# Seventeen of twenty-two gate and up pairs of a SwiGLU block as seven half-size products, with two weight sums made by accumulating transfers

## The chip, the cores and the metric

The kernel runs on one core of one Trainium2 chip. The metric is the device time of one execution in microseconds (us); the kernel before was run three times, and its median is the figure to compare with. A separate, profiled execution left the trace from which every row below is read. TensorE is called PE, VectorE DVE, ScalarE ACT, GpSimd POOL and SyncE SP, as in the profile.

## The reference, cut to what matters

Two transformer blocks run one after the other on 512 tokens of width 1024, all in fp32. Block 1 mixes with a multi-scale pool and a dilated attention and then has a SwiGLU layer of width 2816; block 2 mixes with three attentions and ends with other gated layers. The change is in block 1's SwiGLU, the first half of it:

```python
h = rms_norm(x, ln_pre_ffn[l])
f = (jax.nn.silu(h @ w_gate[l]) * (h @ w_up[l])) @ w_down[l]
x = x + rms_norm(f, ln_post_ffn[l])
```

`h` is 512 x 1024, `w_gate` and `w_up` are 1024 x 2816. The result must hold fp32 accuracy.

## The kernel before

Activations lie transposed: features on the 128 partitions, the 512 tokens along the free axis. The 2816 columns of gate and of up are cut into 22 blocks of 128; block i of gate and block i of up are a pair, and each of the two is a slab: eight chunks of 128 input features, and for each chunk three matmuls, since fp32 accuracy is had from a reduced format (fp32r) by splitting every operand into a high and a low part: high x high, high x low, low x high (`mm3`, L186 to L188). A slab is thus 24 matmuls of 128x128 weights with 128x512 tokens, a pair 48.

Weights come in units of 512 KB (one slab of 128 columns). SP starts the load into one of two buffers of the pool `raw` (L158); ACT makes the high part by a rounding copy (L164), DVE the low part by a subtraction (L167), in two halves of 128x512, into rings of ten buffers each (`NW`). An SP queue runs in order, and a load into a `raw` buffer waits until the parts of the unit before in that buffer are made.

`ffn1` makes the pairs in a loop. The first two pairs (four slabs) are interleaved chunk by chunk and by token halves (`beside`); after that each slab stands by itself. When the slabs of a pair are done, DVE multiplies gate by the row of inverse norms R (L647), ACT applies silu (L112), DVE multiplies up by R (L650) and both together (L651), and the product is split for the down projection (ACT L176, DVE L177) and kept in the slots `p`, `t`, `o`, `k`. R is applied after the matmuls, so that `h` there is not yet normed. The down projection (`post`) follows.

A list scheduler orders the instructions of each engine when the kernel is built; at run time each engine and each queue goes strictly in that order. Slots are named buffer classes with a count (`SLOTS`); PSUM has eight banks of 128x512.

Of the kernel before, what the change touches and what calls it, by code (L numbers as in the profile page):

```python
# [21 lines left out]
EPS = 1e-6  # L22
BIG = 1e30
WH = 524
# [5 lines left out]
NW = 10  # L30
# [12 lines left out]
DONE2 = [0, 1, 2, 3, 4, 5, 6, 7]  # L43
KA2 = 6
BESIDE = 4
NA2 = 4
SLOTS = dict(h=16, o=14, k=16, z=6, v=8, p=8, t=6, m=8)

# [13 lines left out]
class Builder:  # L62
# [118 lines left out]
                lo[:, cols], src[:, cols], scale, hi[:, cols].bitcast(F32), ALU.mult, ALU.subtract)  # L181
        return hi, lo

    def mm3(self, out, ahi, alo, bhi, blo, start, stop):
        mm = self.nc.tensor.matmul
        mm(out, lhsT=ahi, rhs=bhi, start=start, stop=False)  # L186
        mm(out, lhsT=ahi, rhs=blo, start=False, stop=False)  # L187
        mm(out, lhsT=alo, rhs=bhi, start=False, stop=stop)  # L188

    def slab(self, out, name, s, h, order=None, halves=((0, S),), units=None, gate=None, free=0):  # L190
        order = list(range(len(h))) if order is None else order
# [228 lines left out]
    def setup(self):  # L420
        nc = self.nc
        self.res = None
        self.special = []
        self.mark = None
        self.tables("natural_log_exp_and_others")
        io = self.io
        self.cols = self.const("cols", [P, NCOL])
        self.ident = self.const("ident", [P, P])
        self.ones = self.const("ones", [P, P])
        self.eps = self.const("eps", [P, 1])  # L430
        self.one = self.const("one", [P, 1])
        nc.sync.dma_start(self.cols[:, :KD], io["cols"][:, :KD])
        self.rest = lambda: nc.sync.dma_start(self.cols[:, KD:], io["cols"][:, KD:])
        nc.gpsimd.memset(self.ones, 1.0)
        warm = self.psT()
        for _ in range(WARM):
            nc.tensor.matmul(warm[:, 0:P], lhsT=self.ones, rhs=self.ones, start=True, stop=True)
        nc.gpsimd.memset(self.eps, EPS)
        nc.gpsimd.memset(self.one, 1.0)

    def load_x(self, ks=range(KD)):
        x = []
        for k in ks:
            t = self.slot("v")
            self.load_late(t, self.io["x"][k])
            x.append(t)
        return x

# [88 lines left out]
    def pool_branch(self, us, oT):  # L537
        nc = self.nc
        io = self.io
        add = ALU.add  # L540
        hi, lo = self.wunit("w_pool", 0, 1)[0]

        def shift_add(src, k, rows=slice(0, P)):
            t = self.slot("h")
            nc.vector.tensor_tensor(t[rows, k:], src[rows, k:], src[rows, :S - k], add)
            nc.vector.tensor_copy(t[rows, :k], src[rows, :k])
            return t
        for i in range(2):
# [12 lines left out]
            ps = self.psum()  # L561
            c = slice(i * P, i * P + P)
            self.mm3(ps, hi[:, c], lo[:, c], dh, dl, True, True)
            oT[i] = self.split(ps, self.col("pool_scale", i), tag="k")

    def post(self, a, order, wname, gname, nname, rows):
        nc = self.nc
        get = self.units(wname)
        acc = self.slot("z")
        mg = []  # L570
        x = self.res
        H = (slice(0, 256), slice(256, S))
        R = self.slot("z")
        nk = len(a)

        def part(m, cols, gate=None):
            d = self.psum(True)
            if m == len(mg):
                mg.append(self.slot("m"))
            self.slab(d, wname, m, a, order, ((cols.start, cols.stop),), get,  # L580
                      gate, (GATE if nk == KD else GATE2) if m == cut else 0)
            nc.scalar.activation(mg[m][:, cols], d[:, cols], AF.Copy, scale=self.col(gname, m))
            self.square_acc(acc, d, m == 0, cols)
        cut = KD - (NHALF if nk == KD else NHALF2)
        for m in range(cut):
            part(m, slice(0, S))
        if x is None:
            x = self.load_x()
        self.res = x
        h = self.h_tiles()  # L590
# [24 lines left out]

    def h_tiles(self):
        return [(self.slot("h", F32R), self.slot("h", F32R)) for _ in range(KD)]

    def stats(self, rows, tag="z"):
        acc = self.slot(tag)  # L620
# [8 lines left out]
    def ffn1(self, h, R):  # L629
        nc = self.nc  # L630
        self.tables("silu_and_others")
        get = self.units("w_gu1")
        act = []
        for i in range(KF):
            if i == 0:
                early = [self.psum(True) for _ in range(BESIDE)]
                self.beside(early, range(BESIDE), h, ((0, 256), (256, S)), get)
            gu = []
            for s in (2 * i, 2 * i + 1):
                if s < BESIDE:  # L640
# [11 lines left out]
            act.append(self.split(t, **self.act_tiles(i)))  # L652
        self.tables("natural_log_exp_and_others")
        return self.post(act, None, "w_down", "ln_post_ffn", "ln_mix_2", False)

    def mix2(self, h, rc):
        nc = self.nc
# [222 lines left out]
    def ffn2(self, h, R):  # L880
# [113 lines left out]
def _layout(i):  # L994
# [80 lines left out]
```

## Time and profile before

| what | value |
|---|---|
| three runs | 1343.4, 1339.58, 1339.52 us, median 1339.58 us |
| the profiled execution | 1343.58 us, its span 1341.5 us |
| PE busy | 1311.8 us of the span (98%) |
| DVE busy | 851.3 us (63%) |
| ACT busy | 672.6 us (50%) |
| POOL busy | 153.8 us (11%) |
| mean granted TensorE clock | 0.994 of full |
| seventeen pairs that the change touches | 292.4 to 481.6 us after the span's start |

The times are on one axis from the span's start. The span is 2.1 us shorter than its own execution; those 2.1 us lie before the first and after the last instruction. Instructions of one engine overlap a little: the time from one start to the next is what an instruction takes away from its engine, and the duration is longer, as it runs to the last result.

### The profile page before, as it was taken

The page shows a single profiled execution, that of the slowest core. Times are in us where ns is not written, and L with a number is a line of the kernel's source. Part 1 is how long each engine was busy: PE and PEld are TensorE (multiplying, and loading weights), DVE is VectorE, ACT ScalarE, POOL GpSimd, SP SyncE. Part 2 cuts the span into 40 slices and gives each one's busy share as a digit, 9 for nine tenths or more (in the row PEclk, how much of TensorE's full clock was granted, in tenths as well). Part 3 has the DMA queues.
Part 4 walks back from the last instruction along what each step waited for, and adds up shares of the span by engine and source line. Part 5 has one row for each costly group of instructions (what it writes and reads, how often), then busy time and mean ns, then how long its engine had stood idle before and what let it go on. Part 6 is the DMA issues. An engine that isn't in the chain of part 4 may idle for free.

```text
span 1341.5 us, 20064 instructions
## 1 busy us (share of the span) xinstructions
PE 1311.8 (98%) x7450; PEld 1138.0 (85%) x7450; DVE 851.3 (63%) x1771; ACT 672.6 (50%) x1327; POOL 153.8 (11%) x190
## 2 busy tenths in 40 slices
PE   9799999999999999999999999899999999999998
PEld 9799988988888888888988999779888888888887
DVE  7777885864444432229588878766877777733354
ACT  6466755543333332237576777755554444522241
POOL 1232220000000000001222334430000000000000
PEclk9999999999999999999999999999999999999999
DMA  6322334233333333228244445333332332332221
GB/s 228 109 67 68 95 111 126 70 117 96 96 95 95 94 95 94 95 70 262 88 112 117 123 117 138 93 106 124 126 95 95 94 95 94 102 95 94 94 79 63
DMA packets 48801, 141.69 MB, mean 106 GB/s; under 512 B 6240, under 2 KB 7136, under 8 KB 48704
## 3 DMA queue, kind: packets, MB, share of 16 engines
q1 hardware_dynamic: 48704, 140.42, 34.0%
q8 instruction: 58, 0.95, 0.3%
q14 instruction: 39, 0.32, 0.1%
HBM read 122.38 MB, written 6.29 MB: 96 GB/s over the span
## 4 chain that ended last, share of the span: by engine, by line
PE 84%; DVE 8%; DMA 3%; ACT 2%; issue 2%; SPq 1%; POOL 0%; DVEq 0%; ACTq 0%; POOLq 0%
PE p L186 21%; PE p L187 21%; PE p L188 21%; PE p L372 4%; PE p L373 4%; PE p L374 4%; DVE wl L167 2%; PE p L283 2%; PE p L292 1%; PE p L291 1%; PE p L261 1%; DVE sp L265 1%; PE p L262 1%; DMA wr<-in_w_qk 1%; ACT sp L112 1%
## 5 line engine op out<-in xcount | busy, mean ns | idle before, releaser
L164 ACT ACTIVATE wh<-wr 128x512 fp32r<-128x512 f32 x417 | 259.2, 630 | 405.4 <-PE p L187 351.9
L167 DVE TENSOR_TENSOR wl<-wr,wh 128x512 fp32r<-128x512 f32 (+1 forms) x400 | 286.2, 723 | 238.5 <-ACT wh L164 227.1
L188 PE MATMUL p<-sh,wl 128*128 128x512 f32 (+1 forms) x858 | 320.4, 377 | 0.0
L187 PE MATMUL p<-sh,wh 128*128 128x512 f32 (+1 forms) x858 | 319.5, 376 | 0.1
L186 PE MATMUL p<-sh,wh 128*128 128x512 f32 (+1 forms) x858 | 311.0, 375 | 1.0 <-ACT sh L179 0.7
L372 PE MATMUL p<-wh,sh 128*128 128x256 f32 (+1 forms) x672 | 193.3, 289 | 5.8 <-ACT sz L485 3.3
L373 PE MATMUL p<-wl,sh 128*128 128x256 f32 (+1 forms) x672 | 192.1, 287 | 0.3 <-DVE wl L167 0.2
L374 PE MATMUL p<-wh,sh 128*128 128x256 f32 (+1 forms) x672 | 191.2, 286 | 0.0
L187 PEld LDWEIGHTS p<-sh,wh 128*128 128x128 f32 x858 | 161.2, 188 | 32.6 <-issue 0.5
L188 PEld LDWEIGHTS p<-sh,wl 128*128 128x128 f32 x858 | 161.2, 188 | 31.8 <-issue 0.7
L186 PEld LDWEIGHTS p<-sh,wh 128*128 128x128 f32 x858 | 157.2, 188 | 33.4 <-ACT sh L179 1.1
L372 PEld LDWEIGHTS p<-wh,sh 128*128 128x128 f32 x672 | 128.7, 192 | 9.1 <-ACT sz L485 3.6
L373 PEld LDWEIGHTS p<-wl,sh 128*128 128x128 f32 x672 | 128.9, 192 | 1.1 <-DVE wl L167 0.8
L374 PEld LDWEIGHTS p<-wh,sh 128*128 128x128 f32 x672 | 128.6, 192 | 1.1 <-issue 0.5
L273 POOL TENSOR_SCALAR sp<-sp,m 128x128 f32<-128x128 f32 (+1 forms) x112 | 72.0, 647 | 186.3 <-DVE m L269 145.5
L112 ACT ACTIVATE sp<-sp,m 128x128 f32<-128x128 f32 (+3 forms) x128 | 71.5, 560 | 36.4 <-DVE m L265 33.8
L188 PE MATMUL p<-so,wl 128*128 128x512 f32 (+1 forms) x246 | 88.5, 360 | 0.0
L187 PE MATMUL p<-so,wh 128*128 128x512 f32 (+1 forms) x246 | 88.5, 360 | 0.0
L186 PE MATMUL p<-so,wh 128*128 128x512 f32 (+1 forms) x246 | 87.6, 361 | 0.6 <-DVE m L265 0.5
L167 POOL TENSOR_TENSOR wl<-wr,wh 128x512 fp32r<-128x512 f32 (+1 forms) x17 | 23.8, 1402 | 455.3 <-ACT wh L164 443.7
L265 DVE CUSTOM_DVE_ANT_0 sp<-p,sm 128x128 f32<-128x128 f32 (+3 forms) x128 | 60.4, 483 | 17.3 <-PE p L262 13.5
L187 PE MATMUL p<-sk,wh 128*128 128x512 f32 (+1 forms) x184 | 67.1, 365 | 0.0
(205 smaller groups left out, 2138.8 us busy)
## 6 DMA issues: line engine op xcount, KB each, us to landing
wr<-in_w_gu SPq DMA_DIRECT2D x88, 512.0 KB
wr<-in_w_down SPq DMA_DIRECT2D x44, 512.0 KB
wr<-in_w_qk SPq DMA_DIRECT2D x31, 512.0 KB
sk<-sk SPq DMA_DIRECT2D x88, 128.0 KB
wr<-in_w_out SPq DMA_DIRECT2D x12, 512.0 KB
sv<-in_x SPq DMA_DIRECT2D x16, 256.0 KB
wr<-in_w_ple_gate SPq DMA_DIRECT2D x8, 512.0 KB
wr<-in_w_v SPq DMA_DIRECT2D x6, 512.0 KB
```

The costliest lines, as they stand in the source:

```text
L112: i = self.nc.scalar.activation(out, in_, func, **k)
L164: nc.scalar.activation(hi[:, :w], c, AF.Copy)
L167: eng.tensor_tensor(lo[:, :w], c, hi[:, :w].bitcast(F32), ALU.subtract)
L186: mm(out, lhsT=ahi, rhs=bhi, start=start, stop=False)
L187: mm(out, lhsT=ahi, rhs=blo, start=False, stop=False)
L188: mm(out, lhsT=alo, rhs=bhi, start=False, stop=stop)
L265: nc.vector.tensor_tensor_reduce(p[:, :n], ps[:, :n], tab[:, (3 - qb) * P:S], 1.0, 3e38, ALU.add, ALU.min, accum_out=m[:, 0:1])
L273: self.nc.gpsimd.tensor_scalar(p[:, :n], p[:, :n], m[:, 2:3], 1.0, ALU.mult, ALU.mult)
L283: ins = nc.tensor.transpose(pt[:, w:w + P], ps_list[qb][:, kb * P:kb * P + P], self.ident)
L372: mm(d, lhsT=h[k][0][:, a], rhs=hi[:, c], start=k == 0 and (o == 0 or not first), stop=False)
L373: mm(d, lhsT=h[k][0][:, a], rhs=lo[:, c], start=False, stop=False)
L374: mm(d, lhsT=h[k][1][:, a], rhs=hi[:, c], start=False, stop=k == 7 and (o > 0 or not first))
```

## The change

Pairs 0 to 4 (`PLAIN = 5`) stay as they were. Pairs 5 to 21, seventeen of them, are computed by Strassen's scheme in its form with seven products. The two-by-two blocks are: first and second half of the input features (four chunks each), first and second half of the tokens (256 each), and gate against up. Of the weights g1, g2 (halves of gate) and u1, u2 (halves of up) seven left operands are made: g1, s1 = u1 + u2, s2 = s1 + g1, g2, s3 = g1 + u1, u2, s4 = s2 + g2. Of the four quarters of the normed `h` seven right operands are made once for all pairs (`h_forms`). Each product has four chunks of three matmuls of 128x128 weights with 128x256 tokens: 84 matmuls of half width for a pair, in place of 48 of full width. The products are summed partly in PSUM (products 0, 2, 4 and 5 in one bank, 1 and 6 in another, 3 in a third) and partly by DVE on 128x256 blocks.

For every such pair DVE now has seven low parts of 128x512 (`L788`), two sums s2 and s4 (`L779`), five additions or multiplications of 128x256 (L693, L697, L701, L705, L707) and one split; ACT has seven high parts (`L787`), three copies out of PSUM of 128x256, two silus of 128x256 and one split. The sums s1 and s3 are made by transfers: SP loads one addend of 256 KB into a buffer (`L768`), and POOL then starts a transfer of the other addend, 256 KB, that adds into that buffer (`L769`). Gate is loaded whole (512 KB, `L771`) and u2 as 256 KB (`L775`), both into the two `raw` buffers, so that gate always takes the same one. The four buffers s1 to s4 are single and are used by all seventeen pairs. A pair moves 1.79 MB in place of 1.0 MB. `h` is normed ahead of the products in place of R behind them.

Once, during pairs 1 to 3, DVE and ACT make the right operands: 16 products of 128x256 (L738), 8 sums or differences of 128x512 (L747) and 14 splits. To have room, the residual x is written to DRAM (`parked`, eight transfers of 256 KB, L638) and loaded again in `post`; the unnormed `h` of the plain pairs moves to slots `k`, and one result of the pool branch to slots `h`. The scheduler also orders some pieces of block 1's mixing tail and of block 2's attention a little differently.

```diff
-        for i in range(KF):
+        self.parked = self.dp.tile([KD, P, S], F32, tag="parked", name="parked")
+        for m in range(KD):
+            nc.sync.dma_start(self.parked[m], self.res[m])
...
+        for i in range(PLAIN):
...
+            if i == 0:
+                forms, todo = self.h_forms(R)
+                each = -(-len(todo) // (PLAIN - 2))
+            else:
+                for step in todo[(i - 1) * each:i * each]:
+                    step()
+        self.res = None
+        sums = [self.slot("m") for _ in range(4)]
+        late = []
+        for i in range(PLAIN, KF):
+            wf = self.w_forms(2 * i, sums)
+            A, B, C = (self.psum(True) for _ in range(3))
+            half = slice(0, 256)
+            e, f, t = self.slot("z"), self.slot("z"), self.slot("z")
...
+                    self.mm3(out[:, half], hi[:, c], lo[:, c], bh[:, a], bl[:, a], first and k == 0, k == 3, True)
+
+            times(A, 0, True)
+            nc.scalar.activation(e[:, half], A[:, half], AF.Copy)
+            times(C, 1, True)
+            for step in late[:1]:
+                step()
+            times(A, 2)
+            nc.scalar.activation(e[:, 256:], A[:, half], AF.Copy)
+            for step in late[1:]:
+                step()
+            times(B, 3, True)
+            nc.vector.tensor_tensor(t[:, half], B[:, half], e[:, half], ALU.add)
+            self.act(t[:, half], t[:, half], AF.Silu)
+            times(A, 4)
+            nc.scalar.activation(f[:, half], A[:, half], AF.Copy)
+            nc.vector.tensor_tensor(f[:, 256:], C[:, half], f[:, half], ALU.add)
+
+            def left(A=A, t=t, times=times):
+                times(A, 5)
+                nc.vector.tensor_tensor(t[:, half], t[:, half], A[:, half], ALU.mult)
+
+            def right(C=C, t=t, e=e, f=f, times=times, i=i):
+                times(C, 6)
+                nc.vector.tensor_tensor(t[:, 256:], C[:, half], e[:, 256:], ALU.add)
+                self.act(t[:, 256:], t[:, 256:], AF.Silu)
+                nc.vector.tensor_tensor(t[:, 256:], t[:, 256:], f[:, 256:], ALU.mult)
+                act.append(self.split(t, -1.0, **self.act_tiles1(i)))
+            late = [left, right]
...
+    def w_forms(self, u, sums):
+        nc = self.nc
+        gate, up = self.io["w_gu1"][u], self.io["w_gu1"][u + 1]
+        first, second = slice(0, 512), slice(512, 1024)
+        s1, s2, s3, s4 = sums
+        for out, a, b in ((s1, up[:, first], up[:, second]), (s3, gate[:, first], up[:, first])):
+            nc.sync.dma_start(out, a)
+            nc.gpsimd.dma_start(out, b, accum_op=ALU.add)
+        raw = self.wp.tile([P, 2 * WH], F32, tag="raw", name=self.nm("wr"))
+        nc.sync.dma_start(raw[:, :KD * P], gate)
+        g1, g2 = raw[:, first], raw[:, second]
+        raw = self.wp.tile([P, 2 * WH], F32, tag="raw", name=self.nm("wr"))
+        u2 = raw[:, first]
+        nc.sync.dma_start(u2, up[:, second])
+        made = {}
...
+        src = [lambda: g1, lambda: s1, lambda: plus(s2, s1, g1), lambda: g2,
+               lambda: s3, lambda: u2, lambda: plus(s4, s2, g2)]
+        for j, f in enumerate(src):
+            c = f()
+            hi = self.wp.tile([P, WH], F32R, tag="hi", name=self.nm("wh"), bufs=NW)
+            lo = self.wp.tile([P, WH], F32R, tag="lo", name=self.nm("wl"), bufs=NW)
+            nc.scalar.activation(hi[:, :512], c, AF.Copy)
+            nc.vector.tensor_tensor(lo[:, :512], c, hi[:, :512].bitcast(F32), ALU.subtract)
+            made[j] = (hi, lo)
+        return made.get
```

On DVE, in the kernel before, one of the later pairs stands in this order (`p` is a PSUM bank, `wr` a weight unit as loaded, `wh` and `wl` its high and low part, `sm678` the row R):

```order
L650 TENSOR_TENSOR sz742_3595<-p735_3557,sm678_3176 128x512
L167 TENSOR_TENSOR wl782_3770<-wr778_3763,wh781_3769 128x512
L651 TENSOR_TENSOR sz741_3592<-sz741_3592,sz742_3595 128x512
L177 TENSOR_TENSOR sk744_3599<-sz741_3592,sk743_3598 128x512
L167 TENSOR_TENSOR wl786_3801<-wr784_3798,wh785_3800 128x512
L647 TENSOR_TENSOR sz757_3672<-p745_3602,sm678_3176 128x512
L167 TENSOR_TENSOR wl788_3805<-wr784_3798,wh787_3804 128x512
L167 TENSOR_TENSOR wl796_3846<-wr794_3843,wh795_3845 128x512
```

In the changed kernel one of the seventeen pairs stands on DVE in this order (`sm805` is s1, `sm806` s2, `sm807` s3, `sm808` s4, `wr1047` the gate unit of this pair, other `sz` and `p` those of the two pairs before):

```order
L779 TENSOR_TENSOR sm806_3788<-sm805_3787,wr1047_5183 128x512
L788 TENSOR_TENSOR wl1050_5188<-wr1047_5183,wh1049_5187 128x512
L779 TENSOR_TENSOR sm808_3790<-sm806_3788,wr1047_5183 128x512
L705 TENSOR_TENSOR sz996_4796<-p993_4793,sz994_4794 128x256
L788 TENSOR_TENSOR wl1052_5192<-sm805_3787,wh1051_5191 128x512
L707 TENSOR_TENSOR sz996_4796<-sz996_4796,sz995_4795 128x256
L788 TENSOR_TENSOR wl1054_5197<-sm806_3788,wh1053_5196 128x512
L181 SCALAR_TENSOR_TENSOR so1022_5006<-sz996_4796,so1021_5005 128x512
L788 TENSOR_TENSOR wl1056_5201<-wr1047_5183,wh1055_5200 128x512
L697 TENSOR_TENSOR sz1019_4937<-p1017_4935,sz1019_4937 128x256
L693 TENSOR_TENSOR sz1044_5080<-p1040_5076,sz1042_5078 128x256
L788 TENSOR_TENSOR wl1058_5205<-sm807_3789,wh1057_5204 128x512
```

The first reader of s1 and gate stands at the top (L779), the last reader of s1 on DVE is the fifth row, the last reader of gate the ninth (`wl1056`). After three more rows the next pair's L779 follows.

On DVE at the passage from the plain pairs to the seventeen, these rows of the changed kernel stand ahead of the second pair's first low part (`wr809` is the first pair's gate, `wr810` its u2, `wr831` the second pair's gate; L747 and L178 finish right operands, L658 and `st804` are the last plain pair's):

```order
L788 TENSOR_TENSOR wl818_3813<-wr809_3795,wh817_3812 128x512
L788 TENSOR_TENSOR wl820_3817<-sm807_3789,wh819_3816 128x512
L788 TENSOR_TENSOR wl822_3821<-wr810_3797,wh821_3820 128x512
L178 TENSOR_TENSOR sv786_3700<-so783_3695,sv785_3699 128x512
L658 TENSOR_TENSOR sz801_3777<-sz801_3777,sz802_3780 128x512
L779 TENSOR_TENSOR sm808_3790<-sm806_3788,wr809_3795 128x512
L178 TENSOR_TENSOR sv788_3704<-so784_3697,sv787_3703 128x512
L693 TENSOR_TENSOR sz830_3834<-p826_3830,sz828_3832 128x256
L178 TENSOR_TENSOR st804_3784<-sz801_3777,st803_3783 128x512
L788 TENSOR_TENSOR wl824_3826<-sm808_3790,wh823_3825 128x512
L779 TENSOR_TENSOR sm806_3788<-sm805_3787,wr831_3905 128x512
L788 TENSOR_TENSOR wl834_3910<-wr831_3905,wh833_3909 128x512
```

The last reader of the first pair's gate is the sum s4 (`sm808`), the sixth row, and the second pair's first sum and first low part are the last two. From the first plain eviction of the early pairs (L654 of pair 0, L647 in the kernel before) to the last row shown there are 71 rows on DVE: 52 of TENSOR_TENSOR 128x512, two of SCALAR_TENSOR_TENSOR 128x512, 16 of SCALAR_TENSOR_TENSOR 128x256 and one TENSOR_TENSOR 128x256. In the kernel before the same evictions have only the plain pairs' own work and low parts between them.

On SP, whose queue is in order, every row of this stretch was a load of one unit of 512 KB (L158) in the kernel before, the two `raw` buffers by turns. In the changed kernel the order is this (`sm805` s1, `wr855` gate, `sm807` s3, `wr856` u2, and s1 again):

```order
L768 DMA sm805_3787<-in_w_gu1 128x512
L771 DMA wr855_4047<-in_w_gu1 128x1024
L768 DMA sm807_3789<-in_w_gu1 128x512
L775 DMA wr856_4049<-in_w_gu1 128x512
L768 DMA sm805_3787<-in_w_gu1 128x512
```

The first addend of s1 now stands ahead of the gate load in the same queue, and the first addend of s3 between gate and u2. POOL, which had nothing in this stretch, has 34 rows L769 that alternate between s1 (`sm805`) and s3 (`sm807`).

## Rows read from the trace of the kernel before

**Rows 1.** The page, busy time of each engine and the chain that ended last, by engine.

```profile
PE 1311.8 (98%) x7450; PEld 1138.0 (85%) x7450; DVE 851.3 (63%) x1771; ACT 672.6 (50%) x1327; POOL 153.8 (11%) x190
...
PE 84%; DVE 8%; DMA 3%; ACT 2%; issue 2%; SPq 1%; POOL 0%; DVEq 0%; ACTq 0%; POOLq 0%
```

**Rows 2.** Stretches: seventeen pairs, one pair, a run of half-width matmuls.

```profile
core 0: us, PE busy (x) PEld busy (x) DVE busy (x) ACT busy (x) POOL busy (x), PEclk, DMA share, GB/s
292.40:481.60 189.20, 189.20 (x818) 153.55 (x818) 89.25 (x139) 65.98 (x105) 0.00 (x0) 1.00 0.31 95
...
1275.10:1290.33 15.23, 15.23 (x132) 15.23 (x131) 5.71 (x9) 6.28 (x12) 0.00 (x0) 1.00 0.22 70
300.13:311.24 11.11, 11.11 (x49) 9.04 (x48) 5.24 (x8) 3.79 (x6) 0.00 (x0) 1.00 0.32 96
```

**Rows 3.** PE in order of time: start, duration; ends of two runs of matmuls.

```profile
300.13 0.39 PE L187 MATMUL p<-sh,wh 128*128 128x512 f32 x1
...
311.25 0.40 PE L187 MATMUL p<-sh,wh 128*128 128x512 f32 x1
...
1275.09 0.28 PE L186 MATMUL p<-sk,wh 128*128 128x256 f32 x1
...
1290.34 0.28 PE L188 MATMUL p<-so,wl 128*128 128x256 f32 x1
```

**Rows 4.** DVE in order of time: start, duration, idle before.

```profile
268.96 0.68 DVE L647 TENSOR_TENSOR sz<-p,sm 128x512 f32<-128x512 f32 x1
269.56 0.68 DVE L650 TENSOR_TENSOR sz<-p,sm 128x512 f32<-128x512 f32 x1
...
292.43 0.69 DVE L650 TENSOR_TENSOR sz<-p,sm 128x512 f32<-128x512 f32 x1 [1.60 <-PE p L188]
...
246.13 0.42 DVE L604 TENSOR_TENSOR sv<-sv,sm 128x256 f32<-128x256 f32 x1
246.47 0.48 DVE L180 SCALAR_TENSOR_TENSOR sh<-sv,cols,sh 128x256 fp32r<-128x256 f32 x1
246.87 0.42 DVE L601 TENSOR_TENSOR sm<-sm,sz 128x256 f32<-128x256 f32 x1
...
953.38 0.75 DVE L904 SCALAR_TENSOR_TENSOR sz<-sz,cols,sz 128x510 f32<-128x510 f32 x1
954.04 0.75 DVE L902 SCALAR_TENSOR_TENSOR sz<-sz,cols,sz 128x511 f32<-128x511 f32 x1
```

**Rows 5.** Groups of instructions by shape, 269 to 491.7 us: busy, mean ns, idle before.

```profile
L167 DVE TENSOR_TENSOR wl<-wr,wh 128x512 fp32r<-128x512 f32 x83 | 56.9, 687 | 38.5 <-ACT wh L164 38.5
L164 ACT ACTIVATE wh<-wr 128x512 fp32r<-128x512 f32 x81 | 51.1, 632 | 107.5 <-PE p L187 104.2 <-DVE sz L650 1.5 <-DMA wr<-in_w_gu 1.3
```

**Rows 6.** The chain that ended last, its transfers: start, us.

```profile
19.23 3.39 DMA wr<-in_w_qk
...
228.67 3.42 DMA wr<-in_w_gu
616.33 5.13 DMA wr<-in_w_vm
627.94 5.12 DMA kept<-sv
719.20 4.09 DMA wr<-in_w_vf
```

**Rows 7.** Waits: who waited for what: us in total, times, longest.

```profile
POOL sm L765 <- DMA sm<-in_tab_rel: 4.1, 2, 2.8
```

**Rows 8.** The page: the queue of the transfers, share of 16 engines.

```profile
q1 hardware_dynamic: 48704, 140.42, 34.0%
```

**Rows 9.** Stretches before and behind three idle times of PE (columns as in rows 2).

```profile
629.00:634.70 5.70, 3.69 (x26) 3.08 (x25) 5.70 (x13) 3.94 (x10) 1.43 (x1) 1.00 0.86 323
634.80:641.50 6.70, 6.01 (x29) 5.87 (x28) 3.82 (x9) 4.49 (x9) 0.02 (x1) 0.50 0.43 129
```

**Rows 10.** One tile: the issue of its loads on SP, ns.

```profile
L158 SPq DMA_DIRECT2D wr<-in_w_gu x26: 327/328/328, 304.9 to 443.9; - x26
```

More of the change, by code (lines that the diff above doesn't have):

```diff
@@ L45 @@
 BESIDE = 4
+PLAIN = 5
 NA2 = 4
@@ L182, in split, with mm3 @@
         return hi, lo
-    def mm3(self, out, ahi, alo, bhi, blo, start, stop):
+    def mm3(self, out, ahi, alo, bhi, blo, start, stop, open_group=False):
         mm = self.nc.tensor.matmul
-        mm(out, lhsT=ahi, rhs=bhi, start=start, stop=False)
-        mm(out, lhsT=ahi, rhs=blo, start=False, stop=False)
-        mm(out, lhsT=alo, rhs=bhi, start=False, stop=stop)
+        more = dict(skip_group_check=True) if open_group else {}
+        mm(out, lhsT=ahi, rhs=bhi, start=start, stop=False, **more)
+        mm(out, lhsT=ahi, rhs=blo, start=False, stop=False, **more)
+        mm(out, lhsT=alo, rhs=bhi, start=False, stop=stop, **more)
     def slab(self, out, name, s, h, order=None, halves=((0, S),), units=None, gate=None, free=0):
@@ L422, in setup @@
         self.res = None
+        self.parked = None
         self.special = []
@@ L439, in setup, with load_x @@
         nc.gpsimd.memset(self.one, 1.0)
-    def load_x(self, ks=range(KD)):
+    def load_x(self, ks=range(KD), src=None):
         x = []
@@ L444, in load_x @@
             t = self.slot("v")
-            self.load_late(t, self.io["x"][k])
+            self.load_late(t, (self.io["x"] if src is None else src)[k])
             x.append(t)
@@ L563, in pool_branch @@
             self.mm3(ps, hi[:, c], lo[:, c], dh, dl, True, True)
-            oT[i] = self.split(ps, self.col("pool_scale", i), tag="k")
+            oT[i] = self.split(ps, self.col("pool_scale", i), tag="h")
     def post(self, a, order, wname, gname, nname, rows):
@@ L587, in post @@
         if x is None:
-            x = self.load_x()
+            x = self.load_x(src=self.parked)
         self.res = x
-        h = self.h_tiles()
+        h = self.h_tiles("k" if rows else "h")
         gate = None
@@ L614, in post, with h_tiles @@
         return h, self.rstd_cols(side)
-    def h_tiles(self):
-        return [(self.slot("h", F32R), self.slot("h", F32R)) for _ in range(KD)]
+    def h_tiles(self, tag="h"):
+        return [(self.slot(tag, F32R), self.slot(tag, F32R)) for _ in range(KD)]
     def stats(self, rows, tag="z"):
@@ L632, in ffn1 @@
         get = self.units("w_gu1")
+        self.parked = self.dp.tile([KD, P, S], F32, tag="parked", name="parked")
+        for m in range(KD):
+            nc.sync.dma_start(self.parked[m], self.res[m])
         act = []
-        for i in range(KF):
+        todo = []
+        for i in range(PLAIN):
             if i == 0:
@@ L651, in ffn1 @@
             nc.vector.tensor_tensor(t, t, w, ALU.mult)
-            act.append(self.split(t, **self.act_tiles(i)))
+            act.append(self.split(t, **self.act_tiles1(i)))
+            if i == 0:
[7 more added lines that the diff above has]
+        late = []
@@ new lines, in ffn1, with times @@
+        for i in range(PLAIN, KF):
[3 more added lines that the diff above has]
+            e, f, t = self.slot("z"), self.slot("z"), self.slot("z")
+            def times(out, j, first=False, wf=wf):
+                hi, lo = wf(j)
+                for k in range(4):
+                    c = slice(k * P, k * P + P)
+                    a = slice(k % 2 * 256, k % 2 * 256 + 256)
+                    bh, bl = forms[j][k // 2]
+                    self.mm3(out[:, half], hi[:, c], lo[:, c], bh[:, a], bl[:, a], first and k == 0, k == 3, True)
[24 more added lines that the diff above has]
+            late = [left, right]
@@ L653, in ffn1, with act_tiles1, h_forms, form @@
+        for step in late:
+            step()
         self.tables("natural_log_exp_and_others")
         return self.post(act, None, "w_down", "ln_post_ffn", "ln_mix_2", False)
+    def act_tiles1(self, i):
+        tag = ("p" * 4 + "t" * 3 + "o" * 7 + "k" * 8)[i]
+        return dict(hi=self.slot(tag, F32R), lo=self.slot(tag, F32R))
+    def h_forms(self, R):
+        nc = self.nc
+        x = self.res
+        tags = ["h"] * 16 + ["m"] * 4 + ["v"] * 8
+        forms = [[], [], [], [], [], [], []]
+        todo = []
+        quarter = {}
+        def form(j, src, scale=None):
+            for s in src:
+                hi, lo = (self.slot(tags.pop(0), F32R) for _ in range(2))
+                self.split(s, scale, hi, lo)
+                forms[j].append((hi, lo))
+        def normed(a, b):
+            out = [self.slot("o") for _ in range(2)]
+            for k in range(4):
+                m = 4 * a + k
+                c = slice(256 * b, 256 * b + 256)
+                nc.vector.scalar_tensor_tensor(
+                    out[k // 2][:, k % 2 * 256:k % 2 * 256 + 256], x[m][:, c], self.col("ln_pre_ffn", m),
+                    R[:, c], ALU.mult, ALU.mult)
+            quarter[a, b] = out
+        def pair(op, p, q):
+            out = []
+            for u, v in zip(p, q):
+                t = self.slot("o")
+                nc.vector.tensor_tensor(t, u, v, op)
+                out.append(t)
+            return out
+        def keep(name, op, p, q):
+            quarter[name] = pair(op, quarter[p], quarter[q])
+        sub, add = ALU.subtract, ALU.add
+        return forms, [
+            lambda: normed(0, 0), lambda: normed(0, 1), lambda: form(0, quarter[0, 0]),
+            lambda: keep(1, sub, (0, 0), (0, 1)), lambda: form(1, quarter[1]),
+            lambda: normed(1, 1), lambda: keep(2, add, (1, 1), 1), lambda: form(2, quarter[2], -1.0),
+            lambda: keep(3, sub, (1, 1), (0, 1)), lambda: form(4, quarter[3]),
+            lambda: form(6, quarter[1, 1]), lambda: normed(1, 0), lambda: form(3, quarter[1, 0]),
+            lambda: keep(4, sub, 2, (1, 0)), lambda: form(5, quarter[4])]
@@ new lines, in w_forms, with plus @@
+    def w_forms(self, u, sums):
+        nc = self.nc
+        gate, up = self.io["w_gu1"][u], self.io["w_gu1"][u + 1]
[11 more added lines that the diff above has]
+        made = {}
+        def plus(out, a, b):
+            nc.vector.tensor_tensor(out, a, b, ALU.add)
+            return out
+        src = [lambda: g1, lambda: s1, lambda: plus(s2, s1, g1), lambda: g2,
[8 more added lines that the diff above has]
+        return made.get
```

## The prediction

> **What bounds the kernel now.** I read the page first, for the engine that is never idle: PE is busy for 98% of the span, and the chain that ended last runs through PE for 84% of it [rows 1]. Then the stretch that the change touches. In the 189.2 us of the seventeen pairs PE has no idle time at all at full granted clock, while DVE is busy for 89.25 us, ACT for 65.98, POOL for nothing, and the transfers for 0.31 of their engines' time [rows 2]. So here time is won only by giving PE less to do, and everything that the change adds falls on engines that have room. The question is whether that room is enough and whether the new work comes in time.
>
> **What PE saves.** In the timeline 48 matmuls of 512 columns start between 300.13 and 311.25, so one costs 11.12/48 = 0.2317 us and a pair 11.12. A run of 256-column matmuls, each with weights of its own as in the new pairs, makes 131 starts from 1275.09 to 1290.34: 15.25/131 = 0.1164 us [rows 3]. In that run the weight loads were busy all the time too [rows 2], so the price includes them. The new pair is 84 x 0.1164 = 9.8 us. I take 9.83, between this run and slightly slower ones. PE saves 1.30 us a pair, 22.1 us for seventeen, if nothing else sets the pace.
>
> **What DVE and ACT pay.** From one start to the next a 128x512 addition or subtraction costs 0.60 us on DVE, one of 128x256 0.33 to 0.34, a scalar-and-tensor operation 0.40 (256) or 0.66 (512) [rows 4]. A new pair on DVE is seven low parts and two sums (9 x 0.60), one split (0.66) and five of 256 (5 x 0.335): 7.7 us. Counted with full durations, as after a wait (0.69 for 512 [rows 5]), it is about 9.0. ACT has eight copies of 512 at 0.63 [rows 5] and five smaller, about 7.1. Both are below 9.83, so neither alone is the bound; but DVE goes from 47% to about 80% of a pair, and its order is fixed, so it can pass little of a delay by.
>
> **The loops through single buffers.** A new pair needs transfers that can't begin before the pair ahead has finished with the buffer. For s1: DVE's order shows the first reader of s1 (s2 = s1 + g1) at the top and its last reader four rows later; between lie two low parts, s4 and one addition of 256, then the low part itself: 3 x 0.60 + 0.335 + 0.69 = 2.8 us. Then SP loads the first addend, 256 KB, POOL starts the accumulating transfer of the second, 256 KB, and only then can the next pair's s2 start. The one wait for a 256 KB load that I find is 2.8 us [rows 7], which a wait understates where the load began before it. Loads of 512 KB on the chain took 3.39 and 3.42 us with little beside them, 4.09 and 5.13 in loaded places [rows 6]. I take 2.8 for the load and 0.25 for the hand-offs between queues. The loop is then 5.85 + A, where A is the time of one accumulating transfer. The trace has no such transfer and none begun on POOL. From below I bound A by the plain 256 KB, 2.8; from above by 5.13, the slowest 512 KB load, since it reads two sources and writes one. A is nearer to a 256 KB read twice beside other traffic than to either end, so I take the middle, 4.1. The loop is then 10.0 us.
>
> By the page "DMA: Bandwidth & Descriptors" of the Trainium skill (section "Anatomy of one DMA — SWDGE (gpsimd) path") a transfer begun on GpSimd costs about 2.0 us plus its bytes at 436 GB/s, an estimate of 2.6 us for 256 KB; the loop would be 8.5 us, PE would set the pace, and the sum below would be -10.4 in place of -7.5. The page's figure is for a plain transfer, and no trace here shows either kind.
>
> For gate: the last reader of gate is eight rows behind the first, 5 x 0.60 + 2 x 0.335 + 0.66 and the last's own 0.69 make 5.0 us; the load of 512 KB adds 3.4 to 4.1 [rows 6] and the hand-off some 0.2: 8.6 to 9.3, just inside PE's 9.83. s3 is read once, at the twelfth row, and has more room. The traffic itself grows from 95 GB/s (0.31 of the engines) to 1.79 MB in 10 us, 179 GB/s; a stretch of 323 GB/s ran at a share of 0.86 [rows 9], so by this it needs about half, and the queue's mean of 34% over the span [rows 8] leaves room. Four issues of 327 ns on SP [rows 10] are 1.3 us a pair. So the period of a pair is 10.0 us, set by s1's loop with A = 4.1: 17 x (11.13 - 10.0) = **19.2 us won**.
>
> **The passage into the new pairs.** The right operands cost DVE 16 operations of 256, 8 sums and 14 splits, and all stand in one queue with the plain pairs' evictions. From the first plain eviction (268.96 [rows 4]) to s4 of the first new pair there are 64 rows: 16 x 0.40 + 2 x 0.66 + 46 x 0.60 = 35.3 us, so s4 starts at 304.3 and ends at 304.9 at best; every eviction on the way is later than its bank was ready in before, so nothing there waits for PE. s4 is the last reader of the first pair's gate, and the load of the second pair's gate can start only then: it lands at 308.3 to 309. A high part (0.63) and a low part (0.69) later the second pair's first product can start, at about 309.8. PE in its order does five products of the first pair before: the plain pairs end at 292.4 [rows 4], and 5 x 1.40 us bring it to 299.4. It stands idle for about **10 us**, in pieces. From below: if DVE's waits for ACT cost nothing and the load is already under way, 8; from above, with one more load time in the chain, 14.
>
> **The clock.** In before three idle times of PE within 3 us were followed by a stretch at a granted clock of 0.50 for 6.7 us [rows 9]; with 1.2 in place of 2.4 GHz half of it, 3.4 us, was lost. Idle pieces in the passage could bring the same: 0 to 3.4, I take 1.7.
>
> **What I cost at nothing.** Parking the residual: eight writes of 256 KB issue in 2.6 us on SP, ahead of three loads of plain weights, and PE has several units made ahead; uncovered, one such write held the chain for 5.12 us [rows 6]. The reload in `post` starts long before it is needed. Other rows that the scheduler moved in both blocks' mixing parts I cost at 0, with 3 us to either side.
>
> **Sum.** -19.2 + 10 + 1.7 = -7.5 us. The profiled execution of 1343.58 would become 1336.1; it is 4 us above the median of the runs, so the median goes from 1339.58 to **1332.1 us**.
>
> **Rivals.**
> 1. *The accumulating transfer is slow, and s1's loop sets the pace* (slower). Place: the next pair's s2 on DVE, which waits for POOL's transfer, and behind it all low parts and so PE. The saving of a pair is gone, the passage included, when the period reaches 11.13 - 11.7/17 = 10.44, that is A = 4.6. At A = 5.13 the period is 11.0, 17 x 0.15 = 2.6 won and 11.7 lost: +9, 1349. At A = 6 it is 11.85: +24, 1363. For it: two sources, POOL's start, traffic of the gate load at the same time (it is issued between the load and the accumulation). Against: 256 KB is little. 0.32.
> 2. *PE sets the pace*, with A of 3.9 or less: -22.1 + 11.7 = -10.4, 1329.2; and with a passage of 8 us and no clock loss -14, 1325.5. It and the forecast shade into each other; together 0.48.
> 3. *DVE is the bound in fact*: it is four fifths busy, and several of its rows wait for a product of an older pair or for ACT's high part. Each wait that the queue can't make up adds to the period. With 0.4 us a pair above the forecast the period is 10.4: about -1, no difference. 0.15 with the middle values of A.
> 4. *The passage costs little*, because the scheduler's rows overlap better than my count: -20 in all, 1319.6. Against it speak 35 us of DVE rows in one queue. 0.05.
>
> A page speaks against the accumulation in another way: "SBUF — State Buffer" (section "Who interferes with whom") says that a transfer begun on GpSimd can be starved by DVE, as its descriptors are written through a port pair that the two share, but that additions of two tensors take only its read side. By it A would stay as it is, or a little longer; no run so far shows it.
>
> **How the numbers follow.** About 0.3%, 4 us, is what a measurement of this kernel can tell from no change. The forecast and rival 2 lie at -2 to -14 (0.48, of it 0.43 beyond -4); rival 4 adds 0.05 and the lower edge of rival 3 adds 0.02: faster 0.50. Same takes the rest of rival 3 (0.13), the edge of the forecast (0.05) and the low edge of rival 1 (0.02): 0.20. Slower is the rest of rival 1: 0.30. The range goes from 1320 (rival 4) to 1356 (A of about 5.5 in rival 1). For the likeliest case alone it is 1325 to 1338.
>
> **What would show it.** Right: starts of products on PE in the seventeen pairs repeat every 9.8 to 10.2 us, with PE idle mostly once, between 292 and 310, and DVE busy for about 80%. s1's loop as the pace: DVE at L779 waits for a transfer in every pair, and the L769 rows on POOL show A. If DVE is the bound, it has no idle time between rows, while PE waits for low parts at L788. I am wrong if A is beyond 4.6, if the gate load under the new traffic takes over 4.5, or if the passage is far from 10 us.

## The result and the profile after

The changed kernel takes 1372.78 us (median of four runs, 1368.8 to 1374.41) against 1339.89 us for the kernel before: a ratio of 1.023 (95% interval 1.0204 to 1.0255). It is slower by 33 us, where the prediction said 7.5 faster; the time lies above the range. Its profiled span is 1370.1 us against 1341.5.

The page of the changed kernel answers to [rows 1] and [rows 8]. PE's busy time fell by only 3.7 us, its share went from 98% to 95%, and the chain that ended last now holds 9% of the span in transfers into `sm` (s1 and s3). The queue begun on POOL is new, and its issues of 256 KB take a median of 4.4 us to land.

```profile
PE 1308.1 (95%) x8062; PEld 1163.0 (85%) x8062; DVE 919.2 (67%) x1928; ACT 722.0 (53%) x1460; POOL 182.3 (13%) x224
...
PEclk9999999999989999999999999999999999999999
...
q0 software_dynamic: 4896, 8.92, 4.0%
...
PE 70%; DVE 13%; DMA 11%; issue 3%; ACT 2%; POOL 0%; SPq 0%; DVEq 0%; POOLq 0%; ACTq 0%
PE p L188 17%; PE p L190 17%; PE p L189 17%; DMA sm<-in_w_gu 9%; PE p L374 4%; PE p L375 4%; PE p L376 4%; DVE wl L168 2%; PE p L285 2%; DVE wl L788 1%; PE p L294 1%; PE p L293 1%; PE p L263 1%; DVE sp L267 1%; DMA wr<-in_w_gu 1%
...
sm<-in_w_gu POOLq DMA_DIRECT2D x34, 256.0 KB, 4.4
```

By stretches (columns as in [rows 2], whose first row it answers): in the passage PE is busy for 9.47 of 16.3 us, in the stretch of the new pairs, up to the last low part, for 164.87 of 188.8, and the granted clock is 0.94 there. DVE and ACT have room as predicted, and the transfers' share is 0.61.

```profile
293.90:310.20 16.30, 9.47 (x59) 8.46 (x57) 15.49 (x27) 7.83 (x17) 1.73 (x2) 0.90 0.44 113
310.20:499.00 188.80, 164.87 (x1266) 160.32 (x1267) 122.64 (x229) 94.42 (x198) 25.98 (x30) 0.94 0.61 150
```

The waits of that stretch say who is late. DVE waits 15 times at L779 for the transfer into s1, ACT 16 times for `sm` too; the wait for the gate load (`wr`) at L779 is a single one.

```profile
DVE sm L779 <- DMA sm<-in_w_gu: 51.7, 15, 5.5
ACT wh L787 <- DMA sm<-in_w_gu: 40.5, 16, 4.4
...
DVE sm L779 <- DMA wr<-in_w_gu: 0.7, 1, 0.7
```

DVE's timeline at L779 gives the period. Each pair has two such rows, s2 and s4; the s2 rows of the second and the last new pair are the first and the last one here, fifteen periods apart: (490.46 - 308.81)/15 = 12.11 us. The pair before took 11.13, and PE's own work is 9.8.

```profile
308.81 0.69 DVE L779 TENSOR_TENSOR sm<-sm,wr 128x512 f32<-128x512 f32 x1 [0.71 <-DMA wr<-in_w_gu]
...
478.41 0.69 DVE L779 TENSOR_TENSOR sm<-sm,wr 128x512 f32<-128x512 f32 x1 [3.60 <-DMA sm<-in_w_gu]
...
490.46 0.69 DVE L779 TENSOR_TENSOR sm<-sm,wr 128x512 f32<-128x512 f32 x1 [3.60 <-DMA sm<-in_w_gu]
```

The chain through one period shows the loop piece by piece (start, us):

```profile
478.41 0.06 DVE sm L779
...
480.64 0.52 DVE wl L788
481.15 0.11 DVE sz L707
481.26 2.89 DMA sm<-in_w_gu
...
484.19 0.55 issue
484.75 5.63 DMA sm<-in_w_gu
...
490.46 0.06 DVE sm L779
```

From s2 to the end of s1's last reader are 2.85 us, SP's load of the first addend takes 2.89, POOL starts 0.55 later, and the accumulating transfer has landed 5.63 after the start of POOL's instruction: with some hops 12.05 from s2 to s2. Over the fourteen such pieces on the chain from 314.99 to 484.75 the accumulating one takes 5.05 to 7.00, mean 5.98. This is rival 1 of the prediction, nearly as it was written, with A = 6.

### The profile page after: what moved, and what is told of

It is laid out like the page before. It is cut to its first block, busy times and chain, and to the rows that moved or that the text cites. A ratio compares the mean times of both kernels' runs of the same rounds, so it can differ in the third digit from the quotient of the medians.

```text
span 1370.1 us, 21833 instructions
## 1 busy us (share of the span) xinstructions
PE 1308.1 (95%) x8062; PEld 1163.0 (85%) x8062; DVE 919.2 (67%) x1928; ACT 722.0 (53%) x1460; POOL 182.3 (13%) x224
## 3 DMA queue, kind: packets, MB, share of 16 engines
q0 software_dynamic: 4896, 8.92, 4.0%
## 4 chain that ended last, share of the span: by engine, by line
PE 70%; DVE 13%; DMA 11%; issue 3%; ACT 2%; POOL 0%; SPq 0%; DVEq 0%; POOLq 0%; ACTq 0%
PE p L188 17%; PE p L190 17%; PE p L189 17%; DMA sm<-in_w_gu 9%; PE p L374 4%; PE p L375 4%; PE p L376 4%; DVE wl L168 2%; PE p L285 2%; DVE wl L788 1%; PE p L294 1%; PE p L293 1%; PE p L263 1%; DVE sp L267 1%; DMA wr<-in_w_gu 1%
## 5 line engine op out<-in xcount | busy, mean ns | idle before, releaser
L168 DVE TENSOR_TENSOR wl<-wr,wh 128x512 fp32r<-128x512 f32 x332 | 242.0, 739 | 201.0 <-ACT wh L165 191.5
L165 ACT ACTIVATE wh<-wr 128x512 fp32r<-128x512 f32 (+1 forms) x349 | 216.4, 629 | 299.5 <-PE p L189 248.8
L188 PE MATMUL p<-sh,wh 128*128 128x512 f32 (+1 forms) x768 | 263.2, 348 | 17.9 <-DVE sz L705 8.3
L190 PE MATMUL p<-sh,wl 128*128 128x512 f32 (+1 forms) x768 | 264.0, 347 | 11.6 <-DVE wl L788 11.5
L189 PE MATMUL p<-sh,wh 128*128 128x512 f32 (+1 forms) x768 | 263.5, 345 | 0.0
L188 PEld LDWEIGHTS p<-sh,wh 128*128 128x128 f32 x768 | 146.9, 193 | 39.6 <-ACT wh L787 7.2
L190 PEld LDWEIGHTS p<-sh,wl 128*128 128x128 f32 x768 | 147.5, 193 | 31.5 <-DVE wl L788 13.2
L189 PEld LDWEIGHTS p<-sh,wh 128*128 128x128 f32 x768 | 148.0, 193 | 18.2 <-issue 0.2
L374 PEld LDWEIGHTS p<-wh,sh 128*128 128x128 f32 x672 | 127.2, 190 | 8.0 <-ACT sz L488 3.6
L376 PEld LDWEIGHTS p<-wh,sh 128*128 128x128 f32 x672 | 127.0, 190 | 1.3 <-issue 0.5
L190 PE MATMUL p<-sk,wl 128*128 128x512 f32 (+1 forms) x274 | 95.2, 354 | 0.0
L189 PE MATMUL p<-sk,wh 128*128 128x512 f32 (+1 forms) x274 | 95.1, 354 | 0.1
L188 PE MATMUL p<-sk,wh 128*128 128x512 f32 (+1 forms) x274 | 88.4, 355 | 1.9 <-ACT sk L177 1.4
```

Source lines behind the costliest of these rows:

```text
L165: nc.scalar.activation(hi[:, :w], c, AF.Copy)
L168: eng.tensor_tensor(lo[:, :w], c, hi[:, :w].bitcast(F32), ALU.subtract)
L188: mm(out, lhsT=ahi, rhs=bhi, start=start, stop=False, **more)
L189: mm(out, lhsT=ahi, rhs=blo, start=False, stop=False, **more)
L190: mm(out, lhsT=alo, rhs=bhi, start=False, stop=stop, **more)
L374: mm(d, lhsT=h[k][0][:, a], rhs=hi[:, c], start=k == 0 and (o == 0 or not first), stop=False)
```

## The experiments

Theory: s1's loop sets the period. Rival explanations: the traffic as a whole is the limit; DVE and ACT in their fixed order are; the gate buffer is.

**Two buffers for the sums, then for gate too.** The second buffers take `k` slots that are empty until the last results.

```diff
         sums = [self.slot("m") for _ in range(4)]
+        other = [self.slot("k"), sums[1], self.slot("k"), sums[3]]
...
-            wf = self.w_forms(2 * i, sums)
+            wf = self.w_forms(2 * i, sums if i % 2 == 1 else other)
```

> Two buffers each for s1 and s3, by turns from pair to pair (the second ones in k slots that are free until the last pair's result); all transfers, sums and instructions as in the changed kernel. Theory (s1's loop of load, accumulating transfer and readers, 12.1 us in the trace of the changed kernel, sets the period): the period falls to what comes next, PE's 9.8 or the gate buffer's loop of about 9.6 to 10.2, and the time to 1326 to 1338 us. Rival 1 (the transfers themselves are the limit, 1.79 MB a pair with accumulation): the period stays at about 12 and the time at 1365 to 1375. Rival 2 (DVE and ACT, whose rows wait for each other in a fixed order): little changes, 1360 to 1372, and DVE no longer waits for transfers.

Measured: 1335.53 us against 1342.21 for the kernel before in the same session, ratio 0.9957 (0.9942 to 0.9972), so 37 us come back from two buffers alone. The theory holds; neither the traffic nor DVE was the limit.

```diff
+        self.u2 = self.slot("k")
...
-        raw = self.wp.tile([P, 2 * WH], F32, tag="raw", name=self.nm("wr"))
-        u2 = raw[:, first]
+        u2 = self.u2
```

> As e1_two_sum_buffers, and u2 in a slot of its own (a k slot), so that the gate loads use the two raw buffers by turns. Theory: nothing that DVE waits for is a transfer any more, the period is PE's, 9.8 to 9.9, and PE is idle only in the passage, about 8 us: 1324 to 1330 us. Rival 1 (transfers): 1360 or more. Rival 2 (DVE and ACT): as e1_two_sum_buffers within 2 us.

Measured: 1330.9 us, ratio 0.9917 (0.99 to 0.9933): faster than the kernel before by 11 us, and by 4.6 than with two sum buffers alone. The gate buffer can be given little of these 4.6 us. In the kernel with two sum buffers DVE did wait for gate in 13 pairs, but PE was busy for all but 0.5 of the same 158 us (first of the lines below, the second kernel's behind it), and its last half-width matmul starts at 486.67, against 485.42 in the second kernel. So 1.3 us were won in the pairs. The other three came later, in work that this edit does not touch; the kernel with two sum buffers has a granted clock of 0.91 from 600 to 640 and the second kernel 1.00, and why is open.

In the stretches of the second kernel the passage and the seventeen pairs stand apart: behind 312 PE is busy without a gap at full clock, although the transfers' share is 0.75 and 186 GB/s, more than in the changed kernel. Waits of DVE or ACT for a transfer are no longer among the largest; ACT waits for PE to free the buffers of high parts, which is the sign of a bound at PE.

```profile
312.00:470.00 158.00, 157.47 (x1315) 155.64 (x1314) 127.60 (x237) 98.67 (x206) 24.27 (x28) 1.00 0.74 189
...
296.00:312.00 16.00, 10.68 (x64) 9.66 (x63) 15.49 (x28) 10.00 (x20) 2.35 (x3) 0.79 0.68 144
...
312.00:470.00 158.00, 158.00 (x1328) 156.98 (x1328) 132.25 (x241) 101.23 (x206) 24.32 (x28) 1.00 0.75 186
```

```profile
ACT wh L788 <- PE p L189: 43.1, 76, 1.5
DVE wl L789 <- ACT wh L788: 11.8, 25, 0.7
```

Of the 1328 matmuls in these 158 us 23 are 512 wide (by shape); at 0.2317 each they take 5.3 us, which leaves 152.7/1305 = 0.117 for one of 256, against 0.1164 in [rows 3].

**One second buffer at a time.** As the first experiment, with `other` holding a new slot for s3 alone or for s1 alone.

> A second buffer for s3 alone, else as the changed kernel. Theory (s1's loop sets the period): no change, period 12.1, 1365 to 1374 us. If s3's loop, or the two accumulating transfers behind each other on POOL, shared in it, the time falls by 8 us or more.

> A second buffer for s1 alone, else as the changed kernel. s3's loop is then the longest by count: high and low part 1.3, load 2.9, hand-off 0.55, accumulating transfer 6.0, 10.8 us a pair: 1343 to 1351 us. If the gate buffer's loop or PE is longer than that, as e1_two_sum_buffers, 1333 to 1338 us.

Measured: 1364.7 us for s3 alone, 1341.49 for s1 alone (one run each; before 1340.99). s3's buffer alone gives 8 us and s1's alone 31, so s1's loop was the one that set the period; s3's stands next, and its remaining cost (1341.5 against 1335.5 with both) is 6 us. Both times are a little under the ranges expected, 0.3 and 1.5 us. The 8 us just reach what the expectation had named as the sign that s3 shares in the period. The trace of that kernel shows a small share: its chain still goes round s1, with s2 rows from 306.51 to 482.98 in fifteen periods of 11.8 us, and its accumulating transfers into s1 are a little shorter, 4.87 to 6.51, mean 5.75.

**What makes the transfer long.** Three kernels with single buffers as in the changed one. In the first, POOL's transfers are plain copies; in the second, there are none; in the third, gate and u2 are not loaded again.

```diff
-            nc.gpsimd.dma_start(out, b, accum_op=ALU.add)
+            nc.gpsimd.dma_start(out, b)
```

> The changed kernel with the two transfers of a pair that POOL starts being plain copies: the second addend overwrites the first, so s1 and s3 are not sums; every wait, buffer and byte that is loaded stays. If the adding makes the transfer slow, it takes 2.6 to 4.5 us in place of about 6 from load to reader, the loop 8.9 to 10.4, and the time is 1328 to 1346 us. If the start on POOL makes it slow (its issue, 0.86 us, and what follows), it stays at 5 to 6 us and the time at 1355 to 1373.

Measured: 1352.01 us, between the two bands. The queue of this kernel has 2720 packets for the same 8.92 MB, where the accumulating one has 4896, and a median of 3.4 us to land in place of 4.4:

```profile
q0 software_dynamic: 2720, 8.92, 2.1%
...
sm<-in_w_gu POOLq DMA_DIRECT2D x34, 256.0 KB, 3.4
```

One period of its chain is 436.71 - 425.98 = 10.73 us, with 4.37 for the copy begun on POOL beside 2.87 for the load begun on SP, both of 256 KB:

```profile
425.98 0.06 DVE sm L779
...
428.84 2.87 DMA sm<-in_w_gu
...
431.75 0.50 issue
432.25 4.37 DMA sm<-in_w_gu
...
436.71 0.06 DVE sm L779
```

So 1.3 to 1.6 us of A belong to the adding (5.63 to 5.98 against 4.37). The other 1.5, 4.37 against 2.87, look like the price of the start on POOL, but the same trace speaks against that. In the period shown SP begins the loads of gate, of s3's first addend and of u2 at 431.17, 432.43 and 433.53, so the copy into s1 (432.25 to 436.63) has them beside it. The copies into s3 just before and behind it have at first none beside them, later the next load into s1 (428.84 and 439.56), and land within 3.08 and 2.90 us:

```profile
426.68 0.54 POOL L769 DMA_DIRECT2D sm<-in_w_gu  x1 [4.59 <-DMA sm<-in_w_gu]
432.25 0.54 POOL L769 DMA_DIRECT2D sm<-in_w_gu  x1 [5.04 <-DMA sm<-in_w_gu]
437.41 0.54 POOL L769 DMA_DIRECT2D sm<-in_w_gu  x1 [4.62 <-DMA sm<-in_w_gu]
```

Over all seventeen of each the medians are 4.35 us into s1 and 3.15 into s3; in the changed kernel, with the adding, 5.63 and 3.95. The buffer itself is not the reason: the first two copies into s1, which run before these loads come in a row, took 3.43 and 3.17 us, with the adding 3.84 and 4.04. The start on POOL is thus worth some 0.3 us (3.15 against 2.87), the loads beside the transfer 1.2 to 1.7, and the adding 0.8 with little beside it and 1.3 to 1.6 beside the loads.

```diff
-            nc.gpsimd.dma_start(out, b, accum_op=ALU.add)
```

> The changed kernel without the transfers on POOL: s1 and s3 are one addend each (no sums), single buffers and SP's loads as they are. Theory: the loop of s1 is its readers and one load, 5.8 us, so the gate buffer's loop or PE sets the period, 9.8 to 10.2: 1330 to 1337 us. It gives the gate loop by itself: were it the limit beside the accumulation, the time would stay over 1345.

Measured: 1331.77 us (before 1341.46), as the theory has it. With single buffers, but no transfer from POOL, PE is busy for the whole of 312 to 470 at full clock. The gate buffer's loop, without the accumulating transfers beside it, was thus just inside PE's pace, as predicted; DVE waits for gate 12 times, 9.1 us in all, without any effect on PE:

```profile
312.00:470.00 158.00, 158.00 (x1330) 157.03 (x1330) 130.06 (x240) 102.91 (x209) 0.00 (x0) 1.00 0.42 146
```

```profile
DVE sm L778 <- DMA wr<-in_w_gu: 9.1, 12, 1.3
```

```diff
+        if u == 2 * PLAIN:
+            self.kept_raw = [self.wp.tile([P, 2 * WH], F32, tag="raw", name=self.nm("wr")) for _ in range(2)]
...
-        nc.sync.dma_start(raw[:, :KD * P], gate)
+        raw = self.kept_raw[0]
```

> The changed kernel with gate and u2 loaded for the first of the seventeen pairs alone and used again by the others (wrong weights there); s1's and s3's loads and accumulating transfers stay, 1.02 MB a pair less 0.77. What it tells: whether an accumulating transfer takes about 6 us by itself or because it shares the engines with the gate load. By itself: the period stays at 12 and the time at 1360 to 1374. Because of the gate load: about 4 to 4.5 us, the loop about 10, 1330 to 1342.

Measured: 1369.7 us, the time of "by itself", but the reason is not that one. The accumulating pieces on this chain from 330 to 482 take 3.62 to 5.32 us, mean 4.5 of eleven, so about 1.5 us of the 6 did come from sharing the engines with the loads of gate and u2. The period stayed long because in this kernel the scheduler ordered DVE otherwise: s1's last reader now stands three rows lower, behind L701 and two more low parts.

```profile
410.18 0.69 DVE L780 TENSOR_TENSOR sm<-sm,wr 128x512 f32<-128x512 f32 x1 [4.51 <-DMA sm<-in_w_gu]
...
411.39 0.41 DVE L701 TENSOR_TENSOR sz<-sz,p 128x256 f32<-128x256 f32 x1
411.72 0.68 DVE L789 TENSOR_TENSOR wl<-sm,wh 128x512 fp32r<-128x512 f32 x1
...
413.98 0.68 DVE L789 TENSOR_TENSOR wl<-sm,wh 128x512 fp32r<-128x512 f32 x1
...
421.67 0.69 DVE L780 TENSOR_TENSOR sm<-sm,wr 128x512 f32<-128x512 f32 x1 [2.33 <-DMA sm<-in_w_gu]
```

The readers take 414.66 - 410.18 = 4.5 us in place of 2.85, and 4.5 + 2.6 + 0.6 + 4.5 is again 12.2. (The period shown, with a transfer of 3.72, has 11.5.) The expectation had left the order of DVE out. The loop's arithmetic holds; the time alone would have led to the wrong answer.

**The sums on DVE.** Gate and up are loaded whole into the two `raw` buffers, and s1 and s3 are two more additions on DVE; POOL starts nothing.

```diff
-            nc.sync.dma_start(out, a)
-            nc.gpsimd.dma_start(out, b, accum_op=ALU.add)
...
-        src = [lambda: g1, lambda: s1, lambda: plus(s2, s1, g1), lambda: g2,
-               lambda: s3, lambda: u2, lambda: plus(s4, s2, g2)]
+        src = [lambda: g1, lambda: plus(s1, u1, u2), lambda: plus(s2, s1, g1), lambda: g2,
+               lambda: plus(s3, g1, u1), lambda: u2, lambda: plus(s4, s2, g2)]
```

> s1 and s3 as additions on DVE from whole loads of gate and up (512 KB each, the two raw buffers), no transfer from POOL, 1.0 MB a pair. DVE has 1.2 us more a pair, about 8.9 to 9.0. Theory: the period is that of the raw buffers' loops, readers of about 5 to 6 us and a load of 3.4 to 4.5, 9.8 to 10.5, and the time 1328 to 1342 us. Rival 2 (DVE and ACT are the limit already): 1375 us or more. Rival 1 (transfers): as the theory.

Measured: 1347.53 us, ratio 1.0041 (1.0026 to 1.0056), worse than expected by 5 us, yet 25 better than the changed kernel. Its chain runs round up's buffer: 404.59 to 415.63 is one period, 11.0 us, of which 4.48 are the load of 512 KB and 6.5 the twelve rows of DVE between landing and last reader.

```profile
404.59 4.48 DMA wr<-in_w_gu
...
409.10 1.29 DVE sm L776 x2
...
415.01 0.61 DVE wl L785
...
415.63 3.94 DMA wr<-in_w_gu
```

**The passage.** In the second kernel PE saves 22 us in the pairs, and what is lost again is mostly the passage. Two attempts at it, each the second kernel with one edit more:

```diff
-PLAIN = 5
+PLAIN = 7
```

> As e2_and_two_gate_buffers, with seven plain pairs in place of five (15 pairs by products; the right operands are made over five plain pairs in place of three). Theory (what e2_and_two_gate_buffers lacks of 22 us is the passage: DVE's 35 us of rows in one queue, while five plain pairs cover some 23): two pairs fewer cost 2.6 us, the passage's idle time of PE (5.2 us) and the low clock behind it (some 3 us) go, 1322 to 1327 us. Rival (the passage is set by the first loads of the new pairs, which wait for slots of the plain pairs, and moves along with them): 1332 to 1336 us.

Measured: 1328.16 us against 1340.99, ratio 0.9902 (0.9884 to 0.992). It does not stand apart from the second kernel (0.9917), and the median is 1 us above the band. The trace shows the mechanism at work all the same: in 296 to 312 PE is now busy throughout, and in the new passage 2.9 us idle, at full clock.

```profile
296.00:312.00 16.00, 16.00 (x70) 12.96 (x69) 16.00 (x29) 8.68 (x16) 0.33 (x1) 1.00 0.25 83
...
320.00:336.00 16.00, 13.09 (x105) 12.28 (x104) 12.48 (x23) 8.63 (x19) 2.41 (x3) 1.00 0.86 203
```

Its last half-width matmul starts at 482.28, 3.1 us ahead of the second kernel's, but the two spans are the same (1329.4 and 1329.3 us): the gain is lost behind the pairs. This execution has a low clock there that the second kernel's has not (0.91 in 600 to 640 and 0.93 in 700 to 725, against 1.00); whether that is this kernel's order or chance is open.

```diff
-                nc.vector.tensor_tensor(t, u, v, op)
+                nc.gpsimd.tensor_tensor(t, u, v, op)
```

> As e2_and_two_gate_buffers, with the eight sums and differences of the right operands on POOL in place of DVE. Theory (DVE's queue sets the passage): DVE's rows shrink by 8 x 0.60 = 4.8 us, and so does the passage: 1325 to 1329 us. Rival: a sum on POOL takes over twice as long (1.4 us for a low part of the same size in the trace of before), and since the operands build on each other the passage gets no shorter: 1330 to 1337 us.

Measured: 1334.57 us, ratio 0.9948 (0.9929 to 0.9967): slower than the second kernel (0.9917) by 0.3%, though the two intervals just touch, as the rival said. A sum on POOL took 1614 ns against 600 from start to start on DVE [rows 4]. ACT waited for one twice, and PE is busy for 8.49 us from 296 to 312, where it had 10.68 in the second kernel:

```profile
L749 POOL TENSOR_TENSOR so<-so,so 128x512 f32<-128x512 f32 x8 | 12.8, 1614 | 99.5 <-DVE so L740 99.5
...
ACT sh L177 <- POOL so L749: 2.7, 2, 2.1
...
296.00:312.00 16.00, 8.49 (x48) 7.54 (x48) 15.96 (x25) 7.61 (x15) 4.49 (x5) 0.79 0.57 103
```

## Why the prediction was wrong

- **What PE saves** was right. Where nothing else sets the pace (second kernel, and the one without a second addend), PE works without a gap, the seventeen pairs take about 9.8 us each, and the whole is 10 to 11 us faster than before.
- **DVE and ACT** were right: in the second kernel DVE is busy for 132.25 of 158 us, 84% where about 80% was predicted, and PE has no idle time there. The gate buffer's loop, "just inside PE's 9.83", was right too: the kernel without a second addend shows it, and with the accumulating transfers beside it, in the kernel with two sum buffers, PE lacks 0.5 us in 158.
- **The step that failed is "so I take the middle, 4.1"**, the price A of one accumulating transfer. It measured 5.05 to 7.00, mean 5.98, and even the end from above, 5.13, "the slowest 512 KB load", was below it. (The middle of its two ends is 3.97; no sum gives 4.1.) The prediction had named the gate load as traffic beside this transfer, in rival 1, but gave it no price in A. By the experiments A is made of 2.9 for a transfer of this size, some 0.3 for its start on POOL, 1.2 to 1.7 for the loads of gate, s3 and u2 that run beside it, and 1.3 to 1.6 for the adding; with the loads of gate and u2 taken away it is 4.5. Whether DVE's rows hold POOL's transfers up, which the prediction mentioned as well, no run separates.
- **The hand-off** was mis-sized as well: 0.25 predicted, from no row; 0.55 before POOL's start and 0.1 elsewhere measured. Readers (2.8 predicted, 2.85) and load (2.8, 2.89) were right.
- Together they lengthen the period from 10.0 to the measured 12.1 (the pieces of the chain alone, 1.9 and 0.4, would give a little more). 2.1 times 17 is 36 us, from 1332 to 1368. The rival that described this gave 1363 at A = 6, on the right side of its own deciding point (A = 4.6) but with 0.30 for slower. Of the 5 us that 1368 lacks to the measured 1372.78, 4 are no cost of the change: the traced execution of the kernel before lay 4 us above its median, and the prediction took them off. From one traced execution to the other the time rose by 28 us, and the 1336.1 predicted for the traced one becomes 1372 with the 36 and 1369 with the shorter passage below, where it took 1371.83. Some 3 us stay open.
- **The passage** was about right in place and sum: 10 idle and 1.7 for the clock predicted. PE lacks 6.8 us in the changed kernel's row 293.9 to 310.2 and loses 0.10 x 16.3 = 1.6 to the clock; in the second kernel it is 5.3 and 0.21 x 16 = 3.4. So some 8.5 in place of 11.7, in the second kernel with more of it in low clock.
- By the page "DMA: Bandwidth & Descriptors" of the Trainium skill (section "Anatomy of one DMA — SWDGE (gpsimd) path") the prediction had an estimate of 2.6 us for a transfer begun on GpSimd. The trace does not agree: plain ones took 2.85 to 5.20 us from the start on POOL to landing, those into s3 the least, with a median of 3.4, and 4.37 in the loop shown. The measurement decides.

## What to carry to other kernels

Write out a buffer's whole loop (readers, load, second transfer, hand-offs between queues) before putting a transfer behind another into a single buffer: the sum is the period, whatever the shares of the engines say, and a second buffer takes it off the path at no cost in traffic. An operation that the trace does not show should be bounded by the pieces that it is made of, each at its slow end, and with the loads that will run beside it, not by one longer transfer. Where a period is near the deciding point, say so in the chances: here 0.5 us of A lay between gain and loss.

## What the runs showed of the hardware that was not expected

An accumulating transfer of 256 KB occupied POOL for 0.86 us at its issue and took 4.4 us (median) to land, a plain one 0.54 and 3.4. Those with the kernel's other loads beside them were slower (medians into s1 5.63 accumulating and 4.35 plain) than those with little beside them (into s3 3.95 and 3.15). The accumulating ones made 4896 packets of the same 8.92 MB for which the plain ones made 2720. In the second kernel, with more traffic, the accumulating ones took 5.1 to land, and PE still had no idle time behind the passage.
